# Moving every large SBUF tile to a multiple of 1024 bytes in a Conformer layer

## The chip, the cores and the metric

The kernel runs on one core of a Trainium2 chip. The metric is the device time of one execution in microseconds (us), taken as the median of several runs. A core has a matmul engine (PE, TensorE) with a separate path for loading the stationary operand (PEld), a vector engine (DVE), a scalar engine (ACT), GpSimd (POOL), and SP, which only starts transfers here. All five run their own instruction streams and wait for each other through semaphores. SBUF is the memory on the chip that the engines work in; it has 128 partitions, and an address below is a number of bytes within a partition.

## The reference

One layer of a streaming encoder on 256 tokens with 2048 features, in float32:

```python
h = rms_norm(x, ffn1_norm[l])
x = x + MACARON_SCALE * swiglu_ffn(h, ffn1_w_in[l], ffn1_w_out[l])
...
y = jnp.concatenate([rms_norm(ya, out_norm_conv[l]),
                     rms_norm(yb, out_norm_sgu[l])], axis=-1)
x = x + y @ w_mix_out[l]
...
x = x + memory_cross_attention(h, mem_n, w_q[l], w_kv[l], w_o[l])

h = rms_norm(x, ffn2_norm[l])
x = x + MACARON_SCALE * swiglu_ffn(h, ffn2_w_in[l], ffn2_w_out[l])
return rms_norm(x, final_norm)
```

`ya` comes from a gated depthwise convolution, `yb` from a spatial gating unit. An FFN has 5632 hidden features, so its two weight matrices are the largest inputs: about 405 MB are read in all, nearly all of them weights that are used once.

## The kernel before, in words

**Precision.** [...] Each operand is split into a rounded part "hi" and a remainder "lo"; hi x hi, hi x lo and lo x hi are added up in PSUM, the accumulator memory.

**The weight stream.** `weights` (L97 to L109) runs for every tile of weights, 759 times. SP loads 512 KB into `raw`, a ring of four buffers (pool `wraw`). ACT writes hi into `hl`, a ring of three buffers (pool `whl`, L104), and DVE writes lo = raw - hi into the same buffer (L105). Then `raw` is free for the next load, and the matmuls read `hl`. A tile feeds twelve 512-column matmuls, or 14 to 24 matmuls in the products by feature.

**The products.** `by_two` (L252 to L262) is the first FFN product: the activation `x_hl` is stationary, 512 columns of `hl` move. `gemm_n` (L152 to L169) does the same for other products (L163 to L165), among them groups 0 to 2 of the last product (`ffn2_w_out`); group 3 is written out with `by_token` (L807 to L813), its last four weight tiles kept in `held`. `product` (L115 to L118) is used in the products by feature (`ffn1_w_out`, `w_mix_out`, `w_q`, `w_o`): `hl` is stationary, and the activation moves, 512 columns (hi and lo side by side) with the weights' hi at L117 and 256 columns with their lo at L118. `product_joint` (L120 to L125) has three matmuls of 256 columns.

**The activations.** Between the two products of an FFN the 44 blocks of hidden features lie in two tiles: `hA` has blocks 0 to 15, `hB` blocks 16 to 43 (`h_of`, L310). `hA`, like `x_hl`, `y_hl`, `o_hl`, `m_hl` and `held`, comes from the pool `big`, two buffers of 32 KB. `hB` comes from a pool that is opened for the stage.

**Where the tiles lie.** Pools are placed one behind the other in the order in which they are opened, each tile at a multiple of 32 bytes, the first pool at 1152. A program built from the source gives these places:

| tile (pool) | first address | beyond a multiple of 1024 |
|---|---|---|
| ones, ident, pv (const) | 1152, 1664, 2176 | 128, 640, 128 |
| xT (const) | 3648 | 576 |
| x_hl, hA, y_hl, o_hl, m_hl, held (big) | 20032, 52800 | 576 |
| raw (wraw), four buffers | 85568 | 576 |
| hl (whl), three buffers | 101952 | 576 |
| sq, tg, tu (ev) | 126528 | 576 |
| small tiles (st) | 132672 to 144928 | various |
| hB of either FFN; kT | 144928 | 544 |
| q_hl, k_hl, p_hl, v_hl, e (attn) | from 177696 | 544 |
| x2 (ffn2) | 202272 | 544 |
| h (ffn1, gate2); gf; sq2 (late) | 202272 and 218656; 218656; 226848 | 544 |

576 is 64 beyond a multiple of 512; 544 is 32 beyond a multiple of 512. The sizes of the large tiles are multiples of 1024, so all buffers of a pool lie alike. `pv` has 368 numbers (1472 bytes), which is what moves the tiles behind it off; the tiles of `st` add up to 12,256 bytes, 32 less than a multiple of 1024.

**The last product and the end.** After each group of 512 output columns `add_up` (L763 to L769) runs for both token halves: DVE adds half of the accumulator to the residual `x2`, ACT squares the result and sums the squares (its elementwise result goes to a scratch tile, `sq2`, that nobody reads), and POOL multiplies by the final norm's gain. `give` (L771 to L791) turns the sums into the norm's factor, scales the rows and writes them out.

**What sets the order.** The engines' instruction streams are put in order by a scheduler when the program is built, by its own timeline; the buffers of a ring are not handed out strictly in turn. Side work (taps of the convolution and the like) is put between weight tiles by `beside` with written-out costs.

Of the kernel before, what the change touches and what calls it, by code (L numbers as in the profile page):

```python
# [11 lines left out]
F32 = mybir.dt.float32  # L12
F32R = mybir.dt.float32r
AF = mybir.ActivationFunctionType
# [3 lines left out]
P = 128  # L18
# [43 lines left out]
def layer(ctx: ExitStack, tc: tile.TileContext, a: dict):  # L62
    nc = tc.nc
    out = a["out"]

    const = ctx.enter_context(tc.tile_pool(name="const", bufs=1))
    big = ctx.enter_context(tc.tile_pool(name="big", bufs=2))
    wraw = ctx.enter_context(tc.tile_pool(name="wraw", bufs=4))
    whl = ctx.enter_context(tc.tile_pool(name="whl", bufs=3))
    ev = ctx.enter_context(tc.tile_pool(name="ev", bufs=2))  # L70
    st = ctx.enter_context(tc.tile_pool(name="st", bufs=1))
    ps = ctx.enter_context(tc.tile_pool(name="ps", bufs=6, space=bass.MemoryType.PSUM))
    pa = ctx.enter_context(tc.tile_pool(name="pa", bufs=2, space=bass.MemoryType.PSUM))


    later = deque()
# [103 lines left out]
    ident = const.tile([P, P], F32, name="ident")  # L180
    make_identity(nc, ident)
    pv = const.tile([P, NPV], F32, name="pv")
    xT = const.tile([P, KD, T], F32, name="xT")

    def col(name, k):
# [191 lines left out]
    with tc.tile_pool(name="mid", bufs=1) as mid:  # L377
        kT = mid.tile([P, KD, M], F32, name="kT")
        vv = mid.tile([P, 2, D], F32, name="vv")
        with tc.tile_pool(name="mix", bufs=1) as pool:  # L380
# [122 lines left out]
            for n in range(2):  # L503
                acc = gemm_n(a["w_mix_v"][n], lambda k: x_hl[:, k], per=1.35)
                for t in range(2):
                    nc.scalar.activation(
                        out=vs[:, t, n * 512:(n + 1) * 512], in_=acc[t], func=AF.Gelu, scale=r_t[:, t:t + 1]
# [89 lines left out]
            for h in range(HEADS):  # L597
                acc = gemm_n(a["w_v"][h], lambda k: m_hl[:, k], per=1.6)
                for t in range(2):
                    nc.scalar.activation(  # L600
                        out=vv[:, t, h * HD:(h + 1) * HD], in_=acc[t], func=AF.Copy, scale=r_mt[:, t:t + 1]
# [132 lines left out]
    with ExitStack() as stack:  # L734
# [3 lines left out]
        x2 = pool.tile([P, 2, D], F32, name="x2")  # L738
# [16 lines left out]
        late = stack.enter_context(tc.tile_pool(name="late", bufs=1))  # L755
        gf = late.tile([P, D], F32, name="gf")
        nc.sync.dma_start(out=gf, in_=a["final_norm"].partition_broadcast(P))
        sums = st.tile([P, 2, 4], F32, name="sums")
# [4 lines left out]
        def add_up(t, s, acc, i):  # L763
            nc.vector.scalar_tensor_tensor(
                out=x2[:, t, s], in0=acc, scalar=0.5, in1=x2[:, t, s], op0=ALU.mult, op1=ALU.add
            )
            sq = late.tile([P, 512], F32, name="sq2")
            nc.scalar.activation(out=sq, in_=x2[:, t, s], func=AF.Square, accum_out=sums[:, t, i:i + 1])
            nc.gpsimd.tensor_tensor(out=x2[:, t, s], in0=x2[:, t, s], in1=gf[:, s], op=ALU.mult)  # L769

        def give(t, parts):  # L771
# [21 lines left out]
        for n in range(3):  # L793
            acc = gemm_n(a["ffn2_w_out"][n], h) if n else acc_0
            for t in range(2):
                add_up(t, slice(n * 512, (n + 1) * 512), acc[t], n)
# [18 lines left out]
        for i, (k0, kk) in enumerate(parts):  # L815
# [5 lines left out]
            else:  # L821
                kept.append((k0, hi, lo))
        add_up(0, slice(1536, 2048), acc[0], 3)
        give(0, 2)
        for k0, hi, lo in kept:
            by_token(1, k0, hi, lo)
        add_up(1, slice(1536, 2048), acc[1], 3)
        give(1, 4)

# [58 lines left out]
```

## Time and profile before

| | |
|---|---|
| time, median of 3 runs | 2161.44 us (2159.11 to 2161.5) |
| the profiled execution's own time | 2160.25 us |
| its span, first to last instruction | 2158.4 us |
| mean granted TensorE clock | 0.999 |
| matmuls | 11,164 |
| PEld, weight loads busy | 1829.0 us |
| data moved by DMA | 409.95 MB, mean 190 GB/s |
| share of the 16 DMA engines that the main queue took | 62.5% |
| first matmul | 7.33 us after the span's start |

The profile gives each instruction's start and duration, what it waited for, and groups of them by line and by the tiles that they read and write ("acc<-hl,hB" writes an accumulator from `hl` and `hB`; for a matmul the moving operand stands first behind the arrow, then the stationary one). Matmuls are pipelined: a matmul's duration reaches into the next ones, so the distance from one start to the next is shorter than a duration. A stretch ("A:B" in us from the span's start) lists the busy time of each engine in it with the number of instructions, in the order PE, PEld, DVE, ACT, POOL, then the granted clock, the DMA share and GB/s.

### The profile page before, as it was taken

To read this page: it belongs to the slowest core of one execution; us is meant where nothing else is said; L and a number is where in the kernel's file an instruction comes from. 1 tells how busy PE (TensorE), PEld (TensorE's weight loads), DVE (VectorE), ACT (ScalarE), POOL (GpSimd) and SP (SyncE) were. 2 spreads that over 40 slices of the span, in tenths; PEclk is the share of its full clock that TensorE was granted. 3 is DMA by queue.
4 is the path that set the end of the run, shared out by engine and by line. 5 is a ranking of instruction groups with operands and counts; after the bars stand their busy time and mean duration, and the time that the engine had idled before them with its cause. 6 is when DMAs were issued, how large, how long until landed. Compare 5 with 4: busy or idle time off the path is not lost.

```text
span 2158.4 us, 28547 instructions
## 1 busy us (share of the span) xinstructions
PE 2137.0 (99%) x11164; PEld 1829.0 (85%) x11164; DVE 1311.4 (61%) x1705; ACT 996.0 (46%) x1232; POOL 13.3 (1%) x23
## 2 busy tenths in 40 slices
PE   8999999999999999999999999999999999999998
PEld 6788888888888899999888888888888888888886
DVE  5654454555555589888897666766644555444444
ACT  6544444444444453544575454544444444443443
POOL 0000000000000000000000000000000000000000
PEclk9999999999999999999999999999999999999999
DMA  8766666666666676565656653666666656666664
GB/s 276 225 188 192 189 192 183 192 190 181 187 188 188 199 234 193 183 177 185 187 184 195 185 157 118 196 193 186 188 193 187 193 181 193 192 206 192 188 191 149
DMA packets 114759, 409.95 MB, mean 190 GB/s; under 512 B 12864, under 2 KB 12992, under 8 KB 114496
## 3 DMA queue, kind: packets, MB, share of 16 engines
q1 hardware_dynamic: 114336, 407.35, 62.5%
q8 instruction: 87, 1.43, 0.3%
q10 hardware_dynamic: 288, 0.79, 0.1%
q14 instruction: 48, 0.39, 0.0%
HBM read 405.99 MB, written 2.10 MB: 189 GB/s over the span
## 4 chain that ended last, share of the span: by engine, by line
PE 95%; DMA 2%; DVE 1%; issue 1%; ACT 1%; SPq 0%; DVEq 0%; ACTq 0%
PE acc L117 16%; PE acc L258 14%; PE acc L262 14%; PE acc L259 14%; PE acc L118 8%; PE acc L165 5%; PE acc L163 5%; PE acc L164 5%; PE acc L125 3%; PE acc L124 3%; PE acc L123 3%; PE acc L811 1%; PE acc L813 1%; PE acc L812 1%; PE aux L288 1%; DMA raw<-in_x 1%
## 5 line engine op out<-in xcount | busy, mean ns | idle before, releaser
L105 DVE TENSOR_TENSOR hl<-raw,hl 128x1024 fp32r<-128x1024 f32 (+2 forms) x759 | 917.5, 1211 | 775.8 <-ACT hl L104 772.5
L104 ACT CAST hl<-raw 128x1024 fp32r<-128x1024 f32 (+2 forms) x759 | 785.5, 1038 | 1013.5 <-PE acc L262 504.7
L259 PE MATMUL acc<-hl,x_hl 128*128 128x512 f32 x1408 | 446.2, 391 | 0.5 <-DVE hl L105 0.5
L262 PE MATMUL acc<-hl,x_hl 128*128 128x512 f32 x1408 | 440.7, 390 | 0.0
L258 PE MATMUL acc<-hl,x_hl 128*128 128x512 f32 x1408 | 395.3, 393 | 9.7 <-ACT hl L104 8.0
L258 PEld LDWEIGHTS acc<-hl,x_hl 128*128 128x128 f32 x1408 | 261.6, 188 | 62.5 <-ACT hl L104 8.5
L262 PEld LDWEIGHTS acc<-hl,x_hl 128*128 128x128 f32 x1408 | 264.5, 188 | 55.4
L259 PEld LDWEIGHTS acc<-hl,x_hl 128*128 128x128 f32 x1408 | 262.8, 188 | 55.1 <-DVE hl L105 1.4
L117 PE MATMUL acc<-hB,hl 128*128 128x512 f32 x448 | 158.9, 397 | 0.0
L118 PE MATMUL acc<-hB,hl 128*128 128x256 f32 x448 | 125.9, 281 | 0.0
L123 PE MATMUL acc<-x_hl,hl 128*128 128x256 f32 x384 | 108.7, 283 | 0.5 <-ACT hl L104 0.5
L125 PE MATMUL acc<-x_hl,hl 128*128 128x256 f32 x384 | 108.2, 283 | 0.9 <-DVE hl L105 0.7
L124 PE MATMUL acc<-x_hl,hl 128*128 128x256 f32 x384 | 108.5, 283 | 0.0
L117 PEld LDWEIGHTS acc<-hB,hl 128*128 128x128 f32 x448 | 84.1, 188 | 20.4
L117 PE MATMUL acc<-x_hl,hl 128*128 128x512 f32 x256 | 90.6, 396 | 0.0
L117 PE MATMUL acc<-o_hl,hl 128*128 128x512 f32 x256 | 90.2, 398 | 0.0
L117 PE MATMUL acc<-hA,hl 128*128 128x512 f32 x256 | 89.8, 392 | 0.0
L117 PE MATMUL acc<-y_hl,hl 128*128 128x512 f32 x256 | 89.0, 394 | 0.0
L118 PEld LDWEIGHTS acc<-hB,hl 128*128 128x128 f32 x448 | 84.5, 189 | 0.0
L125 PEld LDWEIGHTS acc<-x_hl,hl 128*128 128x128 f32 x384 | 73.4, 192 | 1.3 <-DVE hl L105 1.3
L123 PEld LDWEIGHTS acc<-x_hl,hl 128*128 128x128 f32 x384 | 73.7, 192 | 0.8 <-ACT hl L104 0.7
L124 PEld LDWEIGHTS acc<-x_hl,hl 128*128 128x128 f32 x384 | 73.7, 192 | 0.0
(229 smaller groups left out, 2830.1 us busy)
## 6 DMA issues: line engine op xcount, KB each, us to landing
raw<-in_ffn_w_in SPq DMA_DIRECT2D x352, 512.0 KB, 3.6
raw<-in_ffn_w_out SPq DMA_DIRECT2D x120, 512.0 KB, 3.8
raw<-in_ffn_w_out SPq DMA_DIRECT2D x64, 448.0 KB, 3.5
raw<-in_w_mix_in SPq DMA_DIRECT2D x48, 512.0 KB, 4.6
raw<-in_w_k SPq DMA_DIRECT2D x32, 512.0 KB, 3.8
raw<-in_w_v SPq DMA_DIRECT2D x32, 512.0 KB, 3.7
raw<-in_w_mix_out SPq DMA_DIRECT2D x32, 512.0 KB, 4.5
raw<-in_w_q SPq DMA_DIRECT2D x32, 512.0 KB, 4.5
```

The costliest lines, as they stand in the source:

```text
L104: nc.scalar.copy(out=hl[:, 0, :size], in_=raw[:, :size])
L105: newest[0] = nc.vector.tensor_tensor(out=hl[:, 1, :size], in0=raw[:, :size], in1=hl[:, 0, :size].bitcast(F32), op=ALU.subtract)
L117: nc.tensor.matmul(acc, lhsT=w_hi, rhs=x_hl, start=first, stop=False, skip_group_check=True)
L118: nc.tensor.matmul(acc[:, 0], lhsT=w_lo, rhs=x_hl[:, 0], start=False, stop=last, skip_group_check=True)
L123: nc.tensor.matmul(d, lhsT=w_hi, rhs=x_hl[:, 0], start=first, stop=False, skip_group_check=True)
L124: nc.tensor.matmul(d, lhsT=w_hi, rhs=x_hl[:, 1], start=False, stop=False, skip_group_check=True)
L125: nc.tensor.matmul(d, lhsT=w_lo, rhs=x_hl[:, 0], start=False, stop=last, skip_group_check=True)
L163: nc.tensor.matmul(acc[t], lhsT=x[:, 0, s], rhs=hi[:, k], start=k0 + k == 0, stop=False)
L164: nc.tensor.matmul(acc[t], lhsT=x[:, 0, s], rhs=lo[:, k], start=False, stop=False)
L258: nc.tensor.matmul(acc[t][g], lhsT=x[:, 0, s], rhs=hi[:, c], start=first, stop=False)
L259: nc.tensor.matmul(acc[t][g], lhsT=x[:, 0, s], rhs=lo[:, c], start=False, stop=False)
L262: nc.tensor.matmul(acc[t][g], lhsT=x[:, 1, s], rhs=hi[:, c], start=False, stop=last)
```

## The change

Two filler tiles are allocated that nothing writes or reads, and one scratch tile is replaced.

```diff
     pa = ctx.enter_context(tc.tile_pool(name="pa", bufs=2, space=bass.MemoryType.PSUM))
 
+    st.tile([P, 8], F32, name="to_1024")
+
...
     pv = const.tile([P, NPV], F32, name="pv")
+    const.tile([P, 112], F32, name="to_4096")
     xT = const.tile([P, KD, T], F32, name="xT")
...
-            sq = late.tile([P, 512], F32, name="sq2")
-            nc.scalar.activation(out=sq, in_=x2[:, t, s], func=AF.Square, accum_out=sums[:, t, i:i + 1])
+            sq = wraw.tile([P, 1024], F32, name="raw")
+            nc.scalar.activation(out=sq[:, :512], in_=x2[:, t, s], func=AF.Square, accum_out=sums[:, t, i:i + 1])
```

`to_4096` has 448 bytes: `xT` then begins at 4096, `big` at 20480, `wraw` at 86016, `whl` at 102400 and `ev` at 126976. `to_1024` has 32 bytes and rounds `st` up to 12,288, so that the pools behind it begin at 145408. All of these are multiples of 1024. The small tiles of `st` move too; they stay at multiples of 32. The scratch of the last squares is no longer a tile of its own behind `gf`; each of the eight squares takes a buffer of the ring `raw` and gives it back. No instruction is added or taken away in the source, and no operand changes its size.

## The prediction

> **What bounds the kernel now.** I read the page first: the busy table, the slices, and the chain that ended last.
>
> ```profile
> span 2158.4 us, 28547 instructions
> ...
> PE 2137.0 (99%) x11164; PEld 1829.0 (85%) x11164; DVE 1311.4 (61%) x1705; ACT 996.0 (46%) x1232; POOL 13.3 (1%) x23
> ...
> PEclk9999999999999999999999999999999999999999
> ...
> PE 95%; DMA 2%; DVE 1%; issue 1%; ACT 1%; SPq 0%; DVEq 0%; ACTq 0%
> ```
>
> TensorE is busy for 99% of the span at a full granted clock, and the chain is TensorE for 95% of it. DVE, ACT and the transfers have room. So the change can move the time in three ways: the rate at which matmuls follow each other, new waits of TensorE, and the short start and end. Next I asked for the matmuls that read the two tiles of one FFN activation. hA lies 64 bytes past a multiple of 512, hB 32 bytes past a multiple of 64; every weight tile (hl, held) lies as hA does. The columns are duration min/median/max in ns, then first and last start.
>
> ```profile
> L165 PE MATMUL acc<-hl,hA x96: 389/389/397, 1905.3 to 2049.1; 128*128 128x512 f32 x96
> L813 PE MATMUL acc<-hl,hA x32: 389/389/396, 2089.2 to 2110.0; 128*128 128x512 f32 x32
> ...
> L165 PE MATMUL acc<-hl,hB x168: 389/396/397, 1928.1 to 2088.3; 128*128 128x512 f32 x168
> L813 PE MATMUL acc<-hl,hB x40: 393/395/396, 2110.9 to 2138.0; 128*128 128x512 f32 x40
> L813 PE MATMUL acc<-held,hB x16: 388/394/397, 2138.7 to 2149.2; 128*128 128x512 f32 x16
> ```
>
> The lines are the same, and so are the moving tile and the 512 columns; only the stationary tile differs, and with hB the matmul takes a median of 394 to 396 ns where it takes 389 with hA. Matmuls overlap, so the price is the spacing. That I read from stretches of the timeline that hold one kind alone (the count in brackets takes in the one to three matmuls that run over an edge).
>
> ```profile
> 1966.56:1988.32 21.76, 21.76 (x97) 18.02 (x96) 11.48 (x10) 9.79 (x12) 2.91 (x2) 1.00 0.66 192
> 1988.33:2027.52 39.19, 39.19 (x169) 31.48 (x168) 17.45 (x15) 14.66 (x14) 0.00 (x0) 1.00 0.65 189
> 549.49:555.05 5.56, 5.56 (x34) 4.89 (x33) 3.79 (x7) 2.68 (x4) 0.00 (x0) 1.00 0.64 197
> 555.05:564.93 9.88, 9.88 (x59) 8.59 (x57) 4.61 (x4) 3.98 (x4) 0.00 (x0) 1.00 0.63 182
> 1158.61:1205.76 47.15, 47.15 (x275) 41.24 (x273) 34.55 (x52) 24.30 (x35) 0.00 (x0) 1.00 0.62 190
> 1370.48:1415.72 45.24, 45.24 (x259) 39.21 (x258) 32.27 (x48) 22.53 (x32) 0.00 (x0) 1.00 0.59 188
> ```
>
> First row: 96 matmuls with hA stationary, 21.76 / 96 = 226.7 ns each. Second: 168 with hB, 233.3 ns. TensorE is never idle in either. The other rows are product(), a 512-column and a 256-column matmul in turn with the activation as moving operand: 16 pairs from hA at 347.5 ns, 28 from hB at 352.9, 136 from y_hl at 346.7, 128 from o_hl at 353.4. y_hl and o_hl both lie 64 past 512, like hA, and yet differ by 6.7 ns: in pairs the slow rate comes without the odd 32 bytes as well.
>
> **The change, part by part.**
>
> *hB as stationary operand* (L163 to L165, L811 to L813). Three lines with 168 + 40 + 16 matmuls each are 672. After the change hB begins at a multiple of 1024, and so do hl and held. If the 6.6 ns come from the odd 32 bytes, 672 x 6.6 = 4.4 us go. All of it is on the path, since TensorE has no idle time there. Ends: nothing (the cause is another) and 4.4; I take 4.4, because same line, shape and engine with one tile changed is as near as a row can be.
>
> *hB as moving operand* (L117, L118). 448 pairs (16 features of 28). At the 346.7 ns of y_hl they would give 448 x 6.2 = 2.8 us. But hA and hB are then alike, and all 704 pairs of that product may equally run at the 353.4 of o_hl: 704 x 353.4 = 248.8 us against 16 x 15.44 = 247.0 now, 1.8 slower. I take half the gain, 1.4, since the rows name no reason for either rate. The same coin lies on y_hl and o_hl, 256 pairs each: at most 1.7 us each way. I take 0.
>
> *ACT and DVE on moved tiles.* The split of the same transposed block into hA and into hB shows what 32 odd bytes cost these engines:
>
> ```profile
> L124 PE MATMUL acc<-x_hl,hl 128*128 128x256 f32 x384 | 108.5, 283 | 0.0
> ...
> L113 DVE TENSOR_TENSOR hB<-aux,hB 128x512 fp32r<-128x512 f32 x28 | 18.1, 684 | 0.0
> ...
> L112 ACT CAST hB<-aux 128x512 fp32r<-128x512 f32 x28 | 15.2, 586 | 0.0
> ...
> L113 DVE TENSOR_TENSOR hA<-aux,hA 128x512 fp32r<-128x512 f32 x16 | 10.5, 685 | 0.1
> ...
> L124 PE MATMUL aux<-k_hl,q_hl 128*128 128x256 f32 x32 | 9.0, 282 | 0.0
> ...
> L112 ACT CAST hA<-aux 128x512 fp32r<-128x512 f32 x16 | 8.7, 582 | 0.2 <-PE aux L288 0.2
> ```
>
> 586 against 582 and 684 against 685 ns: nothing, and TensorE hides both. The attention rows are a warning: q_hl and k_hl both lie 32 past 64, and their matmuls take 282 ns against 283 where both lie at 64. So the loss may come from two operands that lie differently rather than from one odd start. Either way the change ends it.
>
> *Square's scratch in the ring of raw.* After groups 0, 1 and 2 of the last product, two squares now need slots of the four that hold loaded weights; after group 3 nothing is loaded any more. Here is the first of these places, ACT, then DVE, then the SP queue's waits and the load's time to landing.
>
> ```profile
> 1963.97 1.05 ACT L104 CAST hl<-raw 128x1024 fp32r<-128x1024 f32 x1 [1.75 <-PE acc L165]
> 1966.76 1.05 ACT L104 CAST hl<-raw 128x1024 fp32r<-128x1024 f32 x1 [1.75 <-PE acc L165]
> 1967.72 0.63 ACT L768 ACTIVATE sq<-x 128x512 f32<-128x512 f32 x1
> ...
> 1968.47 0.63 ACT L768 ACTIVATE sq<-x 128x512 f32<-128x512 f32 x1
> ...
> 1969.48 1.06 ACT L104 CAST hl<-raw 128x1024 fp32r<-128x1024 f32 x1 [0.29 <-PE acc L165]
> ...
> 1974.92 1.05 ACT L104 CAST hl<-raw 128x1024 fp32r<-128x1024 f32 x1 [1.66 <-PE acc L165]
> ```
>
> ```profile
> 1965.05 1.23 DVE L105 TENSOR_TENSOR hl<-raw,hl 128x1024 fp32r<-128x1024 f32 x1 [1.57 <-ACT hl L104]
> 1966.19 1.28 DVE L764 SCALAR_TENSOR_TENSOR x<-acc,x 128x512 f32<-128x512 f32 x2
> 1967.85 1.23 DVE L105 TENSOR_TENSOR hl<-raw,hl 128x1024 fp32r<-128x1024 f32 x1 [0.38 <-ACT hl L104]
> ```
>
> ```profile
> SPq L101 <- DVE hl L105: 18.8, 8, 3.1
> ```
>
> ```profile
> raw<-in_ffn_w_out SPq DMA_DIRECT2D x120, 512.0 KB, 3.8
> ```
>
> Each load starts when a subtraction (L105) frees a slot, and is cast four casts later. The subtraction that ends at 1966.28 frees the slot of the cast at 1974.92: landing at 1966.3 + 3.8 = 1970.1, so 4.8 us to spare. A square that comes ready at about 1967 finds no free slot until the subtraction ends at 1969.08. Two squares in it (0.75 us apart, L768) keep it till about 1970.6, and the load behind them on SP starts 1.5 us late, inside the 4.8. On ACT the cast queued behind the squares (1969.48) slips by about a microsecond; DVE's subtraction and TensorE wait for it, but TensorE works on two ready tiles of 2.72 us. Cost 0, from 0 to the 2.5 us a place of the last rival. POOL's product after each square comes later by the same; it is needed only at the end.
>
> *Start and end.* The rows of weights now land on other bytes. The first matmul waits for its first cast, and no row shows a transfer to an aligned start. I take 0, within 0.3 us either way. The fillers are never read or written.
>
> Sum: 4.4 + 1.4 = 5.8 us off. The profiled execution took 2160.25 (its span 2158.4 and 1.85 around it), so it would be 2154.5; it stood 1.2 below the median of 2161.44. From the median: 2155.6.
>
> **The rivals.**
>
> *Alignment does nothing*: hB is slow for its place or its neighbours. For it: o_hl's pairs, slow at 64. Against it: all 672 stationary uses are slow and none of hA's medians is. Time 2161.4. [...]
>
> *Every matmul gets faster*: y_hl's pair less hA's 512-column matmul, 346.7 - 226.7, leaves 120.0 for 256 columns; so 256 more columns cost 106.7, 512 cost 213.3, and 13.3 ns a matmul are something else. If these are the 64 odd bytes, up to 11,164 x 13.3 = 148 us go, and the time is about 2015. For it: all starts are at 64 or 32, so no row shows an aligned one. Against it: the 13.3 ns are the same at 64 and 64 and (attention) at 32 and 32, which a fixed cost of changing the stationary operand explains as well. [...]
>
> *The ring starves the loads*, which ends slower: slots are handed out in program order, so the square's slot comes ahead of the next group's first load. Then the third tile of that group loads only after the first square, at 1968.4, lands at 1972.2, and is split by 1974.5 (1.05 + 1.23), while TensorE wants it two tiles of 2.72 after 1966.56, at 1972.0: 2.5 us a place, 7.5 in all. With alignment at its weakest (4.4 - 1.8 - 1.7 = 0.9 off) that is 2168. It decides from the point where such a load starts over 4.8 us late. Against it: a load starts 8.6 us before its cast (1966.3 to 1974.92), well ahead of the squares, and need not be ordered behind them.
>
> **How the numbers follow.** Forecast 0.58, nothing 0.19, all matmuls 0.16, ring 0.07. A change within 0.2%, 4.3 us, can't be told from none. Inside the forecast the sum reaches from 4.4 + 2.8 + 1.7 = 8.9 off to 0.9 off, which is 2152.5 to 2160.5; about seven tenths of that lies beyond 4.3. Faster: 0.16 + 0.41 = 0.57. Same: 0.17 + 0.17 = 0.34. Slower: 0.07 and 0.02 of the nothing case with a small ring cost, 0.09. The range leaves out the big gain and most of the ring: from 2161.4 - 8.9 and the 2 to 3 us by which runs spread, 2149, to the nothing case and the same spread, 2164.
>
> **What would show it.** Right: L163 to L165 and L811 to L813 read a median of 389 with hB, the stretch of 168 matmuls takes 38.1 us instead of 39.2, and no idle TensorE follows the squares. Wrong: hB stays at 395 (the place), hA and x_hl fall below 389 (every matmul), or L163 waits for ACT's cast after 1966 (the ring).

## The result, and the profile after

The changed kernel takes a median of 2176.19 us (2174.31 to 2178.42, 4 runs) against 2160.28 us of the kernel before in the same session (2157.71 to 2161.5, 4 runs). The ratio is 1.0079, with a 95% interval from 1.0067 to 1.0091: 15.9 us slower. The forecast was 5.8 us faster, and the sign is wrong. The profiled execution of the changed kernel took 2178.42 us, the longest of its four, so the lines below account for 18.2 us between the two profiles and not for 15.9.

These are the lines of the page of the changed kernel that answer to the first ones of before: span, busy table, chain.

```profile
span 2176.6 us, 28548 instructions
...
PE 2144.6 (99%) x11164; PEld 1834.9 (84%) x11164; DVE 1311.6 (60%) x1705; ACT 994.7 (46%) x1232; POOL 11.9 (1%) x23
...
PE 95%; DMA 2%; ACT 1%; DVE 1%; issue 1%; SPq 0%; DVEq 0%; ACTq 0%
```

On this page almost nothing stands out: the span is 18.2 us longer, the shares are the same, and the slices hide a loss of a few us in each of three places. The rows of hB by line show it (changed kernel; duration min/median/max in ns, then first and last start; all lines are two or three further down than before).

```profile
L120 PE MATMUL acc<-hB,hl x448: 277/281/285, 509.1 to 752.3; 128*128 128x256 f32 x150
...
L167 PE MATMUL acc<-hl,hB x168: 388/389/390, 1930.2 to 2100.0; 128*128 128x512 f32 x168
...
L816 PE MATMUL acc<-hl,hB x40: 389/389/390, 2130.3 to 2156.6; 128*128 128x512 f32 x40
```

With hB stationary the median is now 389 ns, as forecast. Yet the 168 matmuls of L167 reach from 1930.2 to 2100.0, 169.8 us, where the same line took 160.2 before (1928.1 to 2088.3): each single matmul is faster and the stretch is 9.6 us longer. The time is lost between them. Here is TensorE where group 0 of the last product gives way to group 1 (timeline of the changed kernel: start, duration, engine, line, and in brackets the idle time before it and what ended it).

```profile
1967.38 0.39 PE L167 MATMUL acc<-hl,hB 128*128 128x512 f32 x1
1970.30 0.73 PE L165 MATMUL acc<-hl,hA 128*128 128x512 f32 x2 [2.53 <-ACT hl L106]
1972.35 0.80 PE L166 MATMUL acc<-hl,hA 128*128 128x512 f32 x1 [1.32 <-DVE hl L107]
...
1973.38 0.63 PE L166 MATMUL acc<-hl,hA 128*128 128x512 f32 x1
1973.80 0.63 PE L167 MATMUL acc<-hl,hA 128*128 128x512 f32 x1
```

TensorE waits 2.53 us for a cast and 1.32 us for a subtraction, and after that the starts lie 0.42 us apart instead of 0.227. Stretches of the same place show why (length, busy us of PE, PEld, DVE, ACT and POOL with counts, then the granted clock, DMA share, GB/s).

```profile
1964.00:1967.00 3.00, 3.00 (x15) 2.49 (x14) 0.00 (x0) 0.00 (x0) 0.00 (x0) 1.00 0.26 105
...
1972.30:1974.00 1.70, 1.65 (x4) 1.36 (x5) 1.70 (x2) 0.94 (x1) 0.00 (x0) 0.50 0.68 149
1974.00:1977.40 3.40, 3.40 (x10) 2.63 (x9) 0.57 (x1) 0.37 (x1) 0.00 (x0) 0.50 0.91 322
1977.40:1979.00 1.60, 1.60 (x8) 1.29 (x7) 0.89 (x1) 0.67 (x1) 0.00 (x0) 0.84 0.62 238
1979.00:1982.00 3.00, 3.00 (x15) 2.50 (x14) 0.99 (x2) 1.05 (x1) 0.00 (x0) 1.00 0.47 143
```

The granted clock falls from 1.00 to 0.50 and is back only by 1979. The first row also shows DVE and ACT with nothing to do for the 3 us ahead of the border: nobody prepares the next tiles. ACT's timeline says why.

```profile
1956.92 1.05 ACT L106 CAST hl<-raw 128x1024 fp32r<-128x1024 f32 x1 [1.67 <-PE acc L167]
1959.64 1.05 ACT L106 CAST hl<-raw 128x1024 fp32r<-128x1024 f32 x1 [1.67 <-PE acc L167]
1967.85 0.63 ACT L771 ACTIVATE raw<-x 128x512 f32<-128x512 f32 x1 [7.15 <-DVE x L767]
...
1968.59 0.63 ACT L771 ACTIVATE raw<-x 128x512 f32<-128x512 f32 x1
...
1969.22 1.98 ACT L106 CAST hl<-raw 128x1024 fp32r<-128x1024 f32 x2
1972.19 1.05 ACT L106 CAST hl<-raw 128x1024 fp32r<-128x1024 f32 x1 [0.99 <-DMA raw<-in_ffn_w_out]
1977.03 1.05 ACT L106 CAST hl<-raw 128x1024 fp32r<-128x1024 f32 x1 [3.79 <-PE acc L167]
```

Before, three casts of the next group ran ahead of the two squares: this one, then those at 1963.97 and 1966.76, and only then the square at 1967.72.

```profile
1961.17 1.05 ACT L104 CAST hl<-raw 128x1024 fp32r<-128x1024 f32 x1 [1.75 <-PE acc L165]
```

Now the squares stand first in ACT's stream. They need DVE's sum, which needs the group's last matmul, so ACT stands for 7.15 us with the casts behind it that fed TensorE before. TensorE reaches the border with no tile ready. The waits from 1955 to the end add it up over the three borders (engine, line, waited for: us in total, times, longest).

```profile
ACT raw L771 <- DVE x L767: 30.3, 5, 7.2
...
PE acc L165 <- ACT hl L106: 5.1, 2, 2.5
...
PE acc L814 <- ACT hl L106: 4.0, 1, 4.0
...
PE acc L166 <- DVE hl L107: 2.6, 2, 1.3
```

TensorE is idle for 5.1 + 4.0 + 2.6 = 11.7 us. Most of the rest of the loss, below, is the halved clock behind each gap. The other two borders have it too:

```profile
2041.00:2043.00 2.00, 2.00 (x7) 1.57 (x6) 0.50 (x1) 0.00 (x0) 0.00 (x0) 0.56 0.93 342
...
2108.00:2110.00 2.00, 2.00 (x6) 1.57 (x5) 0.00 (x0) 0.00 (x0) 0.00 (x0) 0.50 1.01 363
```

The sum of the profiled executions: in the run that has everything but the loss (the squares called later, below) L167 spans 156.8 us, so two borders cost 169.8 - 156.8 = 13.0. From L167's last hB to L816's first hB it is 30.3 us here and 22.7 there, so the third costs 7.6. Together 20.6. hB as stationary operand gave back 672 x 6.6 = 4.4. The product by feature, where the activation moves, took longer. Here is the 256-column row with hB before, then the 512-column row with hA before and after:

```profile
L118 PE MATMUL acc<-hB,hl x448: 278/280/283, 508.6 to 750.1; 128*128 128x256 f32 x150
...
L117 PE MATMUL acc<-hA,hl x256: 389/391/403, 502.2 to 740.0; 128*128 128x512 f32 x128
...
L119 PE MATMUL acc<-hA,hl x256: 389/398/404, 502.8 to 742.2; 128*128 128x512 f32 x128
```

From the first to the last start with hB, which takes in all of hA's stretches but the first, it was 241.5 us and is 243.2 (509.1 to 752.3), 1.7 more. It is hA's pairs that became slower, whose place beside `hl` did not change: added up from the starts in the two timelines, their 16 stretches take 90.8 us instead of 89.4, and hB's, the last one left out, 148.9 instead of 148.7. 20.6 - 4.4 + 1.7 = 17.9, and the spans differ by 18.2.

### The profile page after: what moved, and what is told of

Its sections match the earlier page's. It is cut to its first block, busy times and chain, and to the rows that moved or that the text cites. A ratio compares the mean times of both kernels' runs of the same rounds, so it can differ in the third digit from the quotient of the medians.

```text
span 2176.6 us, 28548 instructions
## 1 busy us (share of the span) xinstructions
PE 2144.6 (99%) x11164; PEld 1834.9 (84%) x11164; DVE 1311.6 (60%) x1705; ACT 994.7 (46%) x1232; POOL 11.9 (1%) x23
## 4 chain that ended last, share of the span: by engine, by line
PE 95%; DMA 2%; ACT 1%; DVE 1%; issue 1%; SPq 0%; DVEq 0%; ACTq 0%
PE acc L119 16%; PE acc L261 14%; PE acc L262 14%; PE acc L265 14%; PE acc L120 8%; PE acc L166 5%; PE acc L167 5%; PE acc L165 5%; PE acc L127 3%; PE acc L126 3%; PE acc L125 3%; PE acc L814 1%; PE acc L815 1%; PE acc L816 1%; PE aux L291 1%; DMA raw<-in_x 1%
```

## The experiments

Theory: the ring alone costs, because of where it puts the squares on ACT. First rival: it costs through the buffers, that is, loads that start late because squares hold their buffers. Second rival: the moved tiles cost. Twelve kernels were run; "before" was run again beside each set.

| run | median us | before, same session | ratio, 95% interval |
|---|---|---|---|
| ring alone | 2180.18 | 2159.36 | 1.0099 (1.0084 to 1.0114) |
| fillers alone, bfloat16 scratch | 2156.87 | 2159.36 | 0.9988 (0.9979 to 0.9998) |
| changed kernel, squares called later | 2156.72 | 2159.36 | 0.9987 (0.9978 to 0.9996) |
| before, with the new order on ACT | 2180.74 | 2159.36 | 1.0097 (1.0082 to 1.0112) |
| 32-byte filler alone | 2155.79 | 2158.84 | 0.9986 (0.9977 to 0.9995) |
| 448-byte filler alone | 2159.04 | 2158.84 | 1.0003 (0.9993 to 1.0012) |
| all large tiles at odd 32 | 2157.32 | 2158.84 | 0.9992 (0.9983 to 1.0002) |
| hB 64 bytes beyond | 2160.51 | 2158.84 | 1.0009 (1.0 to 1.0019) |
| 512 columns first | 2153.84 | 2158.74 | 0.9979 (0.997 to 0.9988) |
| ring for the last group alone | 2159.14 | 2158.74 | 1.0002 (0.9992 to 1.0012) |
| hB 128 bytes beyond | 2159.79 | 2158.74 | 1.0005 (0.9995 to 1.0014) |
| hB 256 bytes beyond | 2156.71 | 2158.74 | 0.9991 (0.9982 to 1.0001) |

### The two halves of the change

The ring alone, without fillers:

```diff
-            sq = late.tile([P, 512], F32, name="sq2")
-            nc.scalar.activation(out=sq, in_=x2[:, t, s], func=AF.Square, accum_out=sums[:, t, i:i + 1])
+            sq = wraw.tile([P, 1024], F32, name="raw")
+            nc.scalar.activation(out=sq[:, :512], in_=x2[:, t, s], func=AF.Square, accum_out=sums[:, t, i:i + 1])
```

> Only the scratch of the squares is moved into the ring of raw; no fillers, every tile lies as in the kernel before. Theory (the ring alone costs the time): three borders between the groups of the last product lose about 7 us each, 20 us in all, the matmuls with hB as stationary operand keep 233 ns, and the time is about 2180 us, some 4 us above the changed kernel. Rival (the new addresses cost the time): 2160 us, as before.

The fillers alone, with a scratch of its own. The scratch, whose elements nobody reads, is bfloat16 here, half as large, to leave room for the fillers.

```diff
+    st.tile([P, 8], F32, name="st_fill")
...
+    const.tile([P, 112], F32, name="const_fill")
...
-            sq = late.tile([P, 512], F32, name="sq2")
+            sq = late.tile([P, 512], mybir.dt.bfloat16, name="sq2")
```

> Both fillers, and the scratch of the squares stays a tile of its own, in bfloat16 so that it fits beside the fillers (nobody reads it). Theory: hB as stationary operand goes from 233.3 to 226.7 ns (4.4 us off), the pairs of product() on hA and hB run at 353 ns (about 2 us more), no TensorE idle time at the borders: about 2157.5 us. Rival (the new addresses cost the time): about 2176 us.

The ring alone costs 20.8 us, the fillers alone gain 2.5. In the run with the ring alone ACT has the same order as in the changed kernel: the squares stand at 1965.26 and 1966.01, the next group's first casts behind them at 1966.64. The moved tiles are not the cause of the loss.

### The order on ACT, or the buffers

The changed kernel, with the square and POOL's product of a group called only after the third and fourth weight tile of the next group. The ring and the fillers stay.

```diff
+            def squares():
+                sq = wraw.tile([P, 1024], F32, name="raw")
+                nc.scalar.activation(out=sq[:, :512], in_=x2[:, t, s], func=AF.Square, accum_out=sums[:, t, i:i + 1])
+                nc.gpsimd.tensor_tensor(out=x2[:, t, s], in0=x2[:, t, s], in1=gf[:, s], op=ALU.mult)
+
+            return squares
...
+        waiting = []
         for n in range(3):
-            acc = gemm_n(a["ffn2_w_out"][n], h) if n else acc_0
-            for t in range(2):
-                add_up(t, slice(n * 512, (n + 1) * 512), acc[t], n)
+            acc = gemm_n(a["ffn2_w_out"][n], h, between=waiting) if n else acc_0
+            waiting = [add_up(t, slice(n * 512, (n + 1) * 512), acc[t], n) for t in range(2)]
```

> The changed kernel, but the squares of a group (and POOL's product) are called only after the third and fourth weight tile of the next group, so that their buffers of the ring come after those tiles' in program order. Theory (the place in program order decides, not that the ring is shared): no TensorE idle time at the borders, about 2157.5 us. Rival (four buffers are too few for six users): most of the 20 us stay, above 2170 us.

It takes 2156.72 us: the loss is gone with the squares still in the ring. ACT's timeline at the first border and two rows of hB in that run:

```profile
1964.07 1.05 ACT L106 CAST hl<-raw 128x1024 fp32r<-128x1024 f32 x1 [1.67 <-PE acc L167]
1966.79 1.06 ACT L106 CAST hl<-raw 128x1024 fp32r<-128x1024 f32 x1 [1.67 <-PE acc L167]
1967.74 0.63 ACT L773 ACTIVATE raw<-x 128x512 f32<-128x512 f32 x1
...
1968.36 0.62 ACT L773 ACTIVATE raw<-x 128x512 f32<-128x512 f32 x1
...
1969.51 1.06 ACT L106 CAST hl<-raw 128x1024 fp32r<-128x1024 f32 x1 [0.43 <-PE acc L167]
```

```profile
L167 PE MATMUL acc<-hl,hB x168: 389/389/389, 1929.2 to 2086.0; 128*128 128x512 f32 x168
...
L820 PE MATMUL acc<-hl,hB x40: 389/389/389, 2108.7 to 2135.0; 128*128 128x512 f32 x40
```

The casts come first again, and the squares run in the gap where ACT would wait anyway. This run still leaves open whether the order or the loads did it, since later squares also take their buffers later. So the opposite: the kernel before, with its own scratch and its own places, in which the first cast of the next group is told to be issued behind the second square. No square holds a buffer of the ring.

```diff
+    hold = [None]
...
+        if hold[0] is None:
+            nc.scalar.copy(out=hl[:, 0, :size], in_=raw[:, :size])
+        else:
+            with tc.issue_after(hold[0].ins):
+                nc.scalar.copy(out=hl[:, 0, :size], in_=raw[:, :size])
+            hold[0] = None
...
+            square = nc.scalar.activation(out=sq, in_=x2[:, t, s], func=AF.Square, accum_out=sums[:, t, i:i + 1])
+            if i < 3 and t == 1:
+                hold[0] = square
```

> The kernel before with its own scratch tile and its own addresses, but on ACT the first cast of the next group is put behind the second square; the loads are free to run ahead. If the order on ACT costs the time: TensorE idles about 2.6 us at each border and loses some more to a lower clock, in all 10 to 20 us, 2170 to 2180 us. If the buffers of the ring cost it (loads that start late): no more than 2 us, about 2161 us.

It takes 2180.74 us, 21.4 above before. ACT's timeline at the first border, then the waits of TensorE in this run:

```profile
1966.70 0.63 ACT L774 ACTIVATE sq<-x 128x512 f32<-128x512 f32 x1 [7.38 <-DVE x L770]
...
1967.46 0.63 ACT L774 ACTIVATE sq<-x 128x512 f32<-128x512 f32 x1
...
1968.09 1.03 ACT L109 CAST hl<-raw 128x1024 fp32r<-128x1024 f32 x1
```

```profile
PE acc L169 <- ACT hl L109: 5.1, 2, 2.5
...
PE acc L819 <- ACT hl L109: 4.0, 1, 4.0
...
PE acc L170 <- DVE hl L111: 2.3, 2, 1.2
```

The idle times are those of the changed kernel, 5.1 and 4.0 us, then 2.3 for 2.6. The order of three instructions on ACT costs the whole loss by itself; the buffers that the squares hold need not be called upon. The changed kernel does have a late load (its cast at 1972.19 waits 0.99 us for it); the run without one loses as much (its first three casts wait for no load). What a late load would cost by itself, with the casts in front of the squares, was not run. Why the scheduler puts the squares in front once their scratch is in the ring is not shown either; the runs show that it does.

The kernel before, with the ring used for the squares of the last group alone, after which no tile is cast:

```diff
-            sq = late.tile([P, 512], F32, name="sq2")
+            if i == 3:
+                sq = wraw.tile([P, 1024], F32, name="raw")[:, :512]
+            else:
+                sq = late.tile([P, 512], F32, name="sq2")
```

> The kernel before, with the squares of the last group alone in the ring of raw; the squares of the groups 0 to 2 keep their own scratch. Theory 'the ring costs by the order on ACT, where casts of a next group stand behind the squares': no group comes after the last, nothing can be put behind its squares, so the time is that of before, 2158 to 2161, and no idle TensorE at any border. Rival 'the scratch in the ring costs wherever it is (the buffer itself, its place, its write)': a quarter of the 20 us, 5 us more, 2164 to 2166.

It takes 2159.14 us against 2158.74: a scratch in the ring costs nothing where no cast can be put behind it.

### What hB's matmuls depend on

Six kernels are the kernel before with other fillers, and nothing else is touched. `st.tile([P, 8])` moves hB (and the tiles placed behind it) by 32 bytes, so that it lies as hl does; 24, 40 and 72 elements put it 64, 128 and 256 bytes beyond hl's place; `const.tile([P, 112])` puts hl and hA at multiples of 1024 and leaves hB 32 short of one; 8 elements in each of the two pools put all large tiles alike, 32 beyond a multiple of 64.

```diff
+    st.tile([P, 8], F32, name="st_fill")
```

> Only the 32-byte filler: hB and all tiles behind the small ones lie 64 past a multiple of 512, as hl and hA do; nothing lies at a multiple of 1024, and the scratch of the squares stays a tile of its own. Theory (the odd 32 bytes are the cost, 1024 is not needed): hB as stationary operand at 226.7 ns, 4.4 us off, and the pairs of product() at one of their two rates, 2.8 us off to 1.8 us more: 2152 to 2157 us. Rival (a multiple of 1024 is what helps): hB stays at 233 ns, about 2159.5 us.

```diff
+    const.tile([P, 112], F32, name="const_fill")
```

> Only the 448-byte filler: hl, hA and x_hl at multiples of 1024, hB 32 short of a multiple of 1024; scratch as before. Theory (the odd 32 bytes): hB as stationary operand stays at 233 ns, hA and x_hl at 227 ns, time as before, 2158 to 2161 us. Rival (a multiple of 1024 for the moving hl helps by itself): hB falls below 233 ns or x_hl below 226.7 ns.

```diff
+    st.tile([P, 8], F32, name="st_fill")
...
+    const.tile([P, 8], F32, name="const_fill")
```

> 32 bytes in each of the two places: hl, hA, x_hl, hB and all other large tiles lie 32 past a multiple of 64, all alike; scratch as before. If the cost is that two operands lie differently: hB as stationary operand at 226.7 ns and everything else as before, about 2156 us. If an odd start of the stationary operand by itself is the cost: every 512-column matmul with its own activation stationary goes to 233 ns, over 6,000 x 6.6 ns, and the time is about 2200 us.

```diff
+    st.tile([P, 24], F32, name="st_fill")
```

> 96 bytes in the small tiles alone: hl and hA 64 past a multiple of 512, hB 128 past, so the two operands differ by 64 bytes. If only the place within 64 bytes counts: hB as stationary operand at 226.7 ns, 2152 to 2157 us. If the two have to lie alike within 512 or 1024 bytes: hB stays at 233 ns or worse, 2159 us or above.

```diff
+    st.tile([P, 40], F32, name="st_fill")
```

> The kernel before with hB begun 128 bytes past the place of hl and hA in their period of 1024 (with 64 between them the matmul took 396 ns, with 0 it took 389). Theory 'any offset between the moving and the stationary operand below 512 is slow': 672 matmuls stay at 394 to 396, time 2159 to 2161. Rival 'the two have to agree within 128': hB at 389, time 2155 to 2157.

```diff
+    st.tile([P, 72], F32, name="st_fill")
```

> The same with 256 bytes between them. Theory 'any offset below 512 is slow': 394 to 396, time 2159 to 2161. Rival 'they have to agree within 256 (or 128)': hB at 389, time 2155 to 2157. Should 128 be slow and 256 fast, the period is 256; should both be slow, it is 512, since the token halves of one tile, 512 bytes apart, are both fast.

The same row, the third matmul of the group with hB stationary, from each of the six in this order (columns as above).

```profile
L167 PE MATMUL acc<-hl,hB x168: 389/389/389, 1928.7 to 2085.5; 128*128 128x512 f32 x168
```

```profile
L165 PE MATMUL acc<-hl,hB x168: 389/396/397, 1930.1 to 2090.3; 128*128 128x512 f32 x168
```

```profile
L167 PE MATMUL acc<-hl,hB x168: 389/389/389, 1928.5 to 2085.3; 128*128 128x512 f32 x168
```

```profile
L167 PE MATMUL acc<-hl,hB x168: 392/393/398, 1930.7 to 2091.0; 128*128 128x512 f32 x168
```

```profile
L167 PE MATMUL acc<-hl,hB x168: 389/393/404, 1928.0 to 2087.7; 128*128 128x512 f32 x168
```

```profile
L167 PE MATMUL acc<-hl,hB x168: 389/389/389, 1929.6 to 2086.5; 128*128 128x512 f32 x168
```

The stretch from first to last start is the price: 156.8, 160.2, 156.8, 160.3, 159.7 and 156.9 us (before 160.2). What is fast is a distance of 0 or 256 bytes between the starts of the stationary and the moving tile; 32, 64 and 128 bytes cost 2.9 to 3.5 us over 504 matmuls, 5.8 to 6.9 ns each. The third run has both tiles 32 beyond a multiple of 64 and is as fast as any, 156.8 us: the odd start itself costs nothing. With both tiles at a multiple of 1024 (squares called later) it is 156.8 us as well: the multiple of 1024 earns nothing. Two theories fell on the way: that only the place within 64 bytes counts (64 bytes apart is slow), and that any distance below 512 is slow (256 is fast). Distances that were not tried, 96 or 192, stay open, and so does the reason; the runs show the distances and the times only.

The whole of the change's gain is thus had with 32 bytes: 2155.79 us, the first of the six.

### The rate of the pairs

In every run with pairs in turn in which hB lies 0, 64, 128 or 256 bytes beyond hl, hA's pairs went at the slow rate, though their place relative to hl did not change: their 512-column matmuls have a median duration of 398 ns there, and 391 in the kernel before and in the runs with the ring alone, the new order on ACT and the 448-byte filler alone, where hB lies 32 bytes off. In the changed kernel and the one before, that is 90.8 us of stretches against 89.4; hB's own stretches hardly moved, 148.9 against 148.7. This kernel has the fillers and the late squares, and in the products of pairs it runs the 512-column matmuls of a weight tile first and the 256-column ones after them.

```diff
-            (product_joint if joint else product)(acc, hi[:, k], lo[:, k], x_hl(k0 + k), f, l)
...
+            for k in range(kk):
+                nc.tensor.matmul(
+                    acc, lhsT=hi[:, k], rhs=x_hl(k0 + k), start=first and k == 0, stop=False, skip_group_check=True
+                )
+            for k in range(kk):
+                nc.tensor.matmul(
+                    acc[:, 0], lhsT=lo[:, k], rhs=x_hl(k0 + k)[:, 0], start=False, stop=last and k == kk - 1,
+                    skip_group_check=True,
+                )
```

> Both fillers and the late squares as in the run with the squares put late (2156.7), and in the product that alternates 512 and 256 columns (activation moving) the 512-column matmuls of a weight tile now come first, then its 256-column ones. Theory 'the slow pair (353.4 ns against 346.7) is a state of the alternation': with no alternation every matmul goes at the rate it has among its own kind, 226.7 and 120.0, together 346.7 a pair, so the 704 pairs of hA and hB lose 704 x 6.7 = 4.7 us, and the other products of this kind (y_hl, o_hl) up to 256 x 6.7 = 1.7 us each: 2150 to 2152. Rival 'it is the tiles, or the number of weight loads, whatever the order': the pairs stay at 353.4 and the time at 2156 to 2157. Slower than 2157 if the order itself makes TensorE wait for the low half later or earlier than now.

It takes 2153.84 us, the fastest of all: 4.9 us below its own before, where the two versions that keep the pairs in turn were 3.1 and 2.6 below theirs (2155.79 and 2156.72). A stretch of 220 us of that product, first with the pairs in turn (squares called later), then with the 512 columns first:

```profile
520.00:740.00 220.00, 220.00 (x1247) 190.88 (x1246) 118.59 (x143) 94.31 (x113) 0.00 (x0) 1.00 0.64 186
```

```profile
520.00:740.00 220.00, 220.00 (x1262) 193.52 (x1261) 120.26 (x144) 95.23 (x116) 0.00 (x0) 1.00 0.65 189
```

A pair takes 440 / 1247 = 0.3528 us in the first and 440 / 1262 = 0.3487 in the second. That is 2.9 us over 704 pairs and not the 4.7 expected: with fewer changes of width the pairs took less, but 346.7 ns is not reached. Which of the two rates a product in turns falls into is not settled. The ring alone left every address where it was, and o_hl's pairs became fast with it (100.2 us from first to last start of the 512-column matmuls, 1313.6 to 1413.8; before, 101.5, 1313.9 to 1415.4; with the new order on ACT 101.6, 1313.7 to 1415.3): so the place of the tiles is not all of it.

## Why the prediction was wrong

**Stationary hB: right.** 672 matmuls at 389 instead of 395 ns, 4.4 us off, in every run that puts hB alike; 256 bytes apart does it as well. The cause that it preferred, the odd 32 bytes, is wrong; its warning, two operands that lie differently, is what the runs showed: medians of 389 ns with 0 or 256 bytes between the two, of 392 to 398 with 32, 64 or 128. Why the distance matters is not shown.

**Moving hB: wrong in sign, within the bounds.** Half a gain, 1.4 off, was taken from two rates that the rows left open; it came out at the other bound, 1.7 on. The gain was to come from hB's pairs, and theirs moved by 0.2; it is hA's that went slow, the case that the prediction had named for that bound. No row said which, so the half was a toss.

**The ring of raw: the step that failed.** It read "Cost 0", with the cast behind the squares slipping by "about a microsecond" while "TensorE works on two ready tiles". All of that was worked out on the order of ACT's stream in the trace of before, with the squares behind the third cast, as if the order were part of the hardware. It is made anew when the program is built. With the squares' scratch in the ring, the squares stand ahead of the first cast, there are no ready tiles, and it costs 20.6 us in the profiled execution. The prediction applied "slots are handed out in program order" to the loads in its rival, and there found 2.5 us a place; the same question was not asked of ACT. The rival's sign was right, and its late load is in the trace: it had the third tile landing at 1972.2, and that tile's cast starts at 1972.19, after waiting 0.99 us for it. But no wait of TensorE ends on that load, and the run with the order alone has the loss without any square holding a buffer of the ring.

**The price of a gap was missing too.** Even with the order known, 11.7 us of waits would have been booked as 11.7. They cost 20.6, 8.9 more, mainly because the granted clock falls to 0.50 for some 3 to 7 us at a border. By an estimate from the stretches' clocks (TensorE's busy time in each, times the share of the clock that is missing) the slow clock takes about 7.6 of the 8.9; the rest was not traced further. At a clock of 0.50 the matmuls start 0.42 to 0.43 us apart, at 1.00 0.227. At the first border the clock was 0.69 from 1970.30 to 1972.30, after the gap of 2.53 us, and 0.50 after the gap of 1.32 us that followed two matmuls later; at the third a single gap of 4.05 us came with 0.50. How long a gap has to be for that, the runs do not show.

**DVE, ACT, start and end: nothing, as forecast**: from before to the changed kernel a cast of a full weight tile goes from a mean of 1051 to 1049 ns and a subtraction stays at 1227, the first matmul starts at 7.09 us instead of 7.33, and from the last matmul's start to the end of the span it is 9.1 us instead of 9.2. The runs with the tiles moved and the order kept differ from before by the two terms above to within about 1 us. The rival by which every matmul becomes faster falls: hA stays at a median of 389 ns at a multiple of 1024 (changed kernel, 448-byte filler alone).

**Its own sign of failure came true**: "L163 waits for ACT's cast after 1966 (the ring)", at 1970.30 (L165 now).

## What to carry to other kernels

Before a scratch tile is moved into a ring that a prefetching stream uses, ask on every engine which instructions of the stream will stand behind the instruction that writes it; a trace of before shows the order that was, not the one that will be built. Some 4 us of idle TensorE cost 6 to 8 us here, so price it with the slow clock behind it. And if tiles are aligned for 512-column float32r matmuls like those with hB stationary, look at the distance between the starts of the two operands: 0, 256 and 512 bytes apart took 389 ns here, 32, 64 and 128 took 392 to 398; rounding both to 1024 gained nothing more (389).

## What the runs showed of the hardware that was not expected

- A float32r matmul of 512 columns with the activation stationary took 226.7 ns from start to start with the stationary and the moving tile at the same place in a period of 512 bytes (hA, before) and 233.3 with 32 bytes between them (hB, before). By the stretches of hB, 256 bytes apart is within 0.1 us over 504 matmuls of 0 apart, and 32, 64 and 128 take 5.8 to 6.9 ns a matmul more. Where both start made no difference in the three places tried: 156.8 us with both at a multiple of 1024, both 576 and both 608 bytes beyond one.
- Matmuls of 512 and 256 columns in turn went at 346.7 to 353.4 ns a pair at a granted clock of 1.00 (before). The pairs of o_hl, at the same addresses, took 101.5 us from first to last start before and 100.2 with the ring alone. With the widths grouped by weight tile a pair of the product that reads hA and hB took 348.7 ns, against 352.8 in turn.
- After a gap of 2.53 us, two matmuls and a gap of 1.32 the granted clock was 0.50, and it was back at 1.00 by 1979, some 7 us after the second gap's end at 1972.35.
